# A conv-gated trunk on one core: four plain tiles instead of five in each channel mixer, and its first splits moved

## The chip, the cores and the metric

The kernel runs on one core of a Trainium2 chip. The metric is the device time of one execution in microseconds (us).

## The reference

Two layers. Each has a token mixer (layer 0: a chunked mLSTM with gates; layer 1: attention over a band of chunks; both beside attention over a memory) and then a channel mixer, which is where the change lies. All in float32, x being 512 tokens by 1024, `D_FF` 2816 = 22 tiles of 128:

```python
def conv_ffn(h, w_up, conv_w, conv_b, w_down):
    u, g = jnp.split(h @ w_up, 2, axis=-1)
    g = causal_dwconv(g, conv_w, conv_b)
    return (jax.nn.silu(g) * u) @ w_down
...
for l in range(DEPTH):
    ...
    x = x + jnp.concatenate([mix_out, mem_out], axis=-1) @ w_out
    x = x + conv_ffn(rmsnorm(x, norm_ffn_g[l]), ffn_w_up[l], ffn_conv_w[l], ffn_conv_b[l], ffn_w_down[l])
return rmsnorm(x, final_g)
```

## The kernel before

**Products.** x is held transposed, 8 tiles of 128 rows by 512 tokens. A float32 product is made of three TensorE matmuls on a high and a low part of each operand (`mm3`, L194 to L196: high by high, high by low, low by high). A *split* (`split`, L140 and L141) makes the parts: ACT casts the high part, DVE subtracts it from the source for the low part. Raw weights go into three buffers `wr`, their parts into `wh0`, `wl0` and so on in turn.

**The channel mixer** (`channel_mixer`, `ChannelMixer`) computes, for each of the 22 tiles of `D_FF`, a gate and an up product, the convolution on the gate, SiLU, and the product of both; the result is split and kept as `hid`. The first `PLAIN` tiles are *plain*: 24 matmuls for the gate and 24 for the up product, each 512 columns wide. The other tiles are *block* tiles (`later`, `step`): gate and up together as one 2 by 2 block product made of seven half-size products, 12 matmuls of 256 columns each, on sums of weight blocks (class `Forms`) and of blocks of x (method `forms`). The results are combined by copies out of PSUM (L834, L842) and additions on DVE (L845, L857). The products of a step stand in this order: a11, a12, s2, then a down unit, s1, s3, then a second down unit, a22, s4; a11, s2, s3 and a22 share the PSUM bank r1.

**Down units.** The down projection is cut into 32 *units* (`down_products`: four tiles of `hid` onto one tile of x, 12 matmuls of 512 columns into a bank with tag `tr`; ACT copies it out, L777, and GpSimd adds it in DRAM). `UNITS` says which units stand beside which tile: 0 to 3 behind the last plain tile, one each beside the block tiles 5 to 8, two beside each from 9 on.

**The norm** runs beside the first plain tile (`Norm.finish`): squares of x are summed, the sum is split, L299 sums over the rows on TensorE, and L301 to L308 make the row of factors. The first `UNSCALED` = 3 plain tiles take x without that row and scale the result; `forms` meanwhile makes the scaled x, its splits (`ready`) and the sums of its blocks (`sums`).

**Order.** The order of instructions on each engine is set by a scheduler, except for the block tiles from the first step on (a stretch of manual order on PE, ACT and DVE) and for instructions that are *pinned* (`pin`), which keep program order. Each engine works its queue in order. `weave` says how far `forms` advances beside a plain tile, in sixteenths.

Of the kernel before, what the change touches and what calls it, by code (L numbers as in the profile page):

```python
# [10 lines left out]
F32R = mybir.dt.float32r  # L11
# [5 lines left out]
P = 128  # L17
D = 1024
S = 512
# [20 lines left out]

PLAIN, UNSCALED, GROUP, LAST = 5, 3, 4, 6
UNITS = {PLAIN - 1: (0, 1, 2, 3), 5: (None, 4), 6: (None, 5), 7: (None, 6), 8: (None, 7)}
UNITS.update((j, (2 * j - 10, 2 * j - 9)) for j in range(9, 21))

H = S // 2
# [7 lines left out]
def trunk(  # L55
# [34 lines left out]
    def sb(tag, shape, dtype=F32):  # L90
        count[0] += 1
        return pool.tile(shape, dtype, tag=tag, name=f"{tag}{count[0]}", bufs=bufs[tag])

    def ps(tag):
        count[0] += 1
        return psum.tile([P, S], F32, tag=tag, name=f"p{tag}{count[0]}", bufs=pbufs[tag])
# [42 lines left out]
    def split(hi, lo, src, on_act=True, pinned=False):  # L139
        high = A.copy(hi, src) if on_act else V.tensor_copy(hi, src)  # L140
        low = V.tensor_tensor(out=lo, in0=src, in1=f(hi), op=ALU.subtract)  # L141
        if pinned:
            pin(high)
            pin(low)
# [13 lines left out]
    turn = [0]  # L158
# [26 lines left out]
    def weights(*args):  # L185
        return parts(load(*args))

    def rows(w, c0, n, k0=0, k1=None):
        k1 = k1 if k1 is not None else w.shape[0] // P
        return w[k0 * P : k1 * P, c0 : c0 + n].rearrange("(k p) c -> p k c", p=P)  # L190
# [4 lines left out]
        nc.tensor.matmul(o, lh, rl, start=False, stop=False, skip_group_check=more)  # L195
        nc.tensor.matmul(o, ll, rh, start=False, stop=last, skip_group_check=more)  # L196

    def project(w, c0, act, tag="mm"):


        n = len(act)
        wh, wl = weights(rows(w, c0, P), n, P)
        o = ps(tag)
        for k in range(n):
            mm3(o, wh[:, k, :], wl[:, k, :], act[k][0], act[k][1], k == 0, k == n - 1)
            yield
        return o

    def run(gen):
        while True:  # L210
            try:
                next(gen)
            except StopIteration as end:
                return end.value
# [10 lines left out]
    def weave(job, filler, each, lead=0):  # L225

        due = lead
        for n in chain([0], job):
            due += each if n is None else each * n
            while due >= 1:  # L230
                due -= 1
                next(filler, None)
# [43 lines left out]
    class Norm:  # L276
# [14 lines left out]
        def finish(self):  # L291


            parts = [sb("t", [P, S], F32R) for _ in range(2)]
            split(*parts, self.acc)
            yield 7.4
            o = ps("sc")
            for i, part in enumerate(parts):
                nc.tensor.matmul(o, onesr, part, start=i == 0, stop=i == 1)  # L299
            v, r, t = sb("rb", [P, S]), sb("t", [P, S]), sb("t", [P, S])  # L300
            A.activation(t, o, AF.Ln, scale=1.0 / D, bias=eps)  # L301
            V.tensor_scalar(v, o, 1.0 / D, EPS, op0=ALU.mult, op1=ALU.add)
            A.activation(r, t, AF.Exp, scale=-0.5)
            A.activation(t, r, AF.Square)
            yield 4
            V.scalar_tensor_tensor(t, t, -0.5, v, op0=ALU.mult, op1=ALU.mult)
            self.row = sb("rb", [P, S])
            V.scalar_tensor_tensor(self.row, t, 1.5, r, op0=ALU.add, op1=ALU.mult)  # L308
# [138 lines left out]
    with tc.manual_schedule(engines={mybir.EngineType.PE, mybir.EngineType.Activation, mybir.EngineType.DVE}):  # L447

        w = ps("mm")
# [215 lines left out]
    class ChannelMixer:  # L665
# [35 lines left out]
        def plain(self, j):  # L701
            scale = self.norm.row if j < UNSCALED else None
            act = self.act if j < UNSCALED else self.ready
            gate = project(self.w, DFF + j * P, act)
            up = project(self.w, j * P, act, "sc")
            if self.norm.row is None:
                both = pair_of(gate, up)
                weave(self.norm.finish(), both, 1)
                og, ou = yield from both
                scale = self.norm.row  # L710
            else:
                og = yield from gate
                ou = None
            acc = sb("t", [P, S])
            src = og
            if scale is not None:
                src = sb("t", [P, S])
                V.tensor_tensor(out=src, in0=og, in1=scale, op=ALU.mult)
            self.last_tap(j, acc, src)
            for _ in self.taps(j, acc, src):  # L720
                pass
            A.activation(acc, acc, AF.Silu)
            if scale is not None:
                V.tensor_mul(acc, acc, scale)
            if ou is None:
                ou = yield from up
            V.tensor_tensor(out=acc, in0=ou, in1=acc, op=ALU.mult)
            self.keep(acc)

        def forms(self):  # L730

            for j in range(KT):
                V.scalar_tensor_tensor(
                    xT[j], xT[j], self.gain[:, j : j + 1], self.norm.row, op0=ALU.mult, op1=ALU.mult
                )
                hi, lo = sb("u", [P, S], F32R), sb("u", [P, S], F32R)
                split(hi, lo, xT[j])
                self.ready.append((hi, lo))
                yield
            self.sums = []  # L740
            for k in range(KT // 2):
                b1, b2 = xT[k], xT[k + KT // 2]
                forms = []
                ta, tb = sb("t", [P, S]), sb("t", [P, S])
                for o, x, y in (
                    (ta[:, :H], b1[:, H:], b1[:, :H]),
                    (ta[:, H:], b2[:, H:], ta[:, :H]),
                    (tb[:, :H], b2[:, H:], b1[:, H:]),
                    (tb[:, H:], b2[:, :H], ta[:, H:]),
                ):  # L750
                    V.tensor_tensor(out=o, in0=x, in1=y, op=ALU.subtract)
                for t in (ta, tb):
                    for h in (t[:, :H], t[:, H:]):
                        both = sb("u", [P, S], F32R)
                        split(both[:, :H], both[:, H:], h)
                        forms.append(both)
                self.sums.append(forms)
                yield

# [3 lines left out]
            g, jj = divmod(q, KT // 2)  # L763
            return load(rows(ffn_w_down[self.l], 2 * jj * P, 2 * P, GROUP * g, GROUP * (g + 1)), GROUP, 2 * P)

        def down_products(self, u):
            g, j = divmod(u, KT)
            w = self.down[u // 2]
            o = ps("tr")
            c = slice(u % 2 * P, (u % 2 + 1) * P)  # L770
            for k in range(GROUP):
                mm3(o, w[0][:, k, c], w[1][:, k, c], *self.hid[GROUP * g + k], k == 0, k == GROUP - 1)
            return j, o

# [25 lines left out]

        def t(self, i):

            return [(p[i - 1][:, :H], p[i - 1][:, H:]) for p in self.sums]

        def later(self):


            prep, tail = Forms(self, PLAIN), None
            prep.split_up()
            prep.sums()  # L810
            prep.split_second()
            prep.sum_third()
            prep.split_sums()
            prep.sum_fourth()
            prep.split_down()
            prep.split_gate()
            with tc.manual_schedule(
                engines={mybir.EngineType.PE, mybir.EngineType.Activation, mybir.EngineType.DVE}
            ):
                for j in range(PLAIN, FT):  # L820
                    self.beside()
                    tail, prep = self.step(j, prep, Forms(self, j + 1) if j + 1 < FT else None, tail)
            for part in (tail.last_block, tail.first_tap, tail.second_tap, tail.third_tap, tail.gated, tail.split):
                part()
# [133 lines left out]
    def channel_mixer(l, act, norm, gain, beside):  # L958

        mixer = ChannelMixer(l, act, norm, gain, beside)  # L960
        forms = mixer.forms()
        run(mixer.plain(0))
        skips = -(turn[0] + 1) % 3
        for j in range(1, UNSCALED):
            turn[0] += j <= skips
            weave(mixer.plain(j), forms, KT / (16.0 * (UNSCALED - 1)))
        until(lambda: len(mixer.ready) == KT, forms)
        mixer.buffers()
        for j in range(UNSCALED, PLAIN):
            units = UNITS.get(j, ())  # L970
            raws = {u // 2: mixer.load_down(u // 2) for u in units[::2]}
            weave(mixer.plain(j), forms, 4 / (16.0 * (PLAIN - UNSCALED)))
            for u in units:
                if u // 2 not in mixer.down:
                    mixer.down[u // 2] = parts(raws[u // 2])
                mixer.add(*mixer.down_products(u))
        run(forms)
        mixer.later()
        reload_x()
        return mixer.hid[FT - LAST :]  # L980

# [556 lines left out]
```

## Time and profile before

| | |
|---|---|
| runs | 1180.72, 1180.85, 1180.89 us (median 1180.85) |
| the profiled execution's own time | 1181.04 us |
| its span | 1179.3 us |
| granted TensorE clock, mean | 0.999 |
| PE busy | 1169.1 us, 99%, 7007 matmuls |
| DVE busy | 935.7 us, 79% |
| ACT busy | 725.8 us, 62% |

Rows of a timeline read: start, length, engine, line, operation, what is written from what with its size, and in brackets the idle time before it and what ended that. An instruction's length overlaps the next one's start, so what an engine can do in a row is told by the distance of the starts. The first channel mixer of layer 0 starts its plain tiles at about 275 us, that of layer 1 at about 830 us.

### The profile page before, as it was taken

How to read it: one execution, taken by the hardware profiler on the slowest of the kernel's cores; microseconds unless marked ns; L12 is line 12 of the kernel's file. 1: busy time of each engine (PE TensorE's matmuls, PEld its weight loads, DVE VectorE, ACT ScalarE, POOL GpSimd, SP SyncE). 2: the span in 40 equal slices, each digit the busy share in tenths (PEclk: the TensorE clock that was granted, in tenths of full speed). 3: DMA queues.
4: the chain of work that ended last, by engine and by line, in shares of the span. 5: the costliest groups of instructions: out<-in, count | busy, mean ns of one | idle time of the engine just before them, and what ended most of it. 6: DMA issues, size and time to landing. Idle time of an engine off the chain costs nothing.

```text
span 1179.3 us, 18676 instructions
## 1 busy us (share of the span) xinstructions
PE 1169.1 (99%) x7007; PEld 1034.2 (88%) x7007; DVE 935.7 (79%) x1688; ACT 725.8 (62%) x1294; POOL 129.9 (11%) x222
## 2 busy tenths in 40 slices
PE   9999999999999999999999999999999999999997
PEld 9988888888889999999888888888889999999986
DVE  6877788887978877777698888897897877777755
ACT  6548677654655655555666667776565655555545
POOL 1111101000021111111020000101001011111100
PEclk9999999999999999999999999999999999999999
DMA  8645325244266677765564312335426466666551
GB/s 299 208 109 134 94 55 152 76 139 121 90 166 163 164 164 162 164 148 129 150 200 125 90 54 85 106 102 177 139 90 153 108 143 144 143 143 141 123 158 72
DMA packets 200156, 158.64 MB, mean 135 GB/s; under 512 B 8344, under 2 KB 179838, under 8 KB 200066
## 3 DMA queue, kind: packets, MB, share of 16 engines
q1 hardware_dynamic: 183906, 119.74, 34.6%
q0 software_dynamic: 15584, 36.67, 16.4%
q8 instruction: 55, 0.90, 0.3%
q10 hardware_dynamic: 576, 1.05, 0.2%
q14 instruction: 35, 0.29, 0.1%
HBM read 128.89 MB, written 32.46 MB: 137 GB/s over the span
## 4 chain that ended last, share of the span: by engine, by line
PE 94%; DVE 3%; ACT 1%; issue 0%; DMA 0%; SPq 0%; POOL 0%; ACTq 0%; POOLq 0%; DVEq 0%
PE pmm L194 18%; PE pmm L195 18%; PE pmm L196 18%; PE ptr L195 6%; PE ptr L194 6%; PE ptr L196 6%; PE psc L195 5%; PE psc L196 5%; PE psc L194 5%; PE psc L544 2%; PE ptr L1365 1%; PE ptr L1386 1%; PE ptr L1387 1%; PE ptr L627 1%; PE ptr L613 0%; DVE pt L141 0%
## 5 line engine op out<-in xcount | busy, mean ns | idle before, releaser
L194 PE MATMUL pmm<-u,wh 128*128 128x512 f32 (+1 forms) x968 | 333.2, 345 | 0.4 <-ACT u L140 0.2
L196 PE MATMUL pmm<-u,wl 128*128 128x512 f32 (+1 forms) x968 | 330.8, 342 | 0.0
L195 PE MATMUL pmm<-u,wh 128*128 128x512 f32 (+1 forms) x968 | 330.5, 342 | 0.0
L141 DVE TENSOR_TENSOR wl<-wr,wh 128x1024 fp32r<-128x1024 f32 (+3 forms) x172 | 199.6, 1162 | 101.8 <-ACT wh L140 101.4
L140 ACT CAST wh<-wr 128x1024 fp32r<-128x1024 f32 (+3 forms) x172 | 172.0, 1002 | 92.7 <-PE pmm L195 39.0
L196 PEld LDWEIGHTS pmm<-u,wl 128*128 128x128 f32 x968 | 181.9, 188 | 20.6
L194 PEld LDWEIGHTS pmm<-u,wh 128*128 128x128 f32 x968 | 181.8, 188 | 19.3 <-ACT u L140 1.1
L195 PEld LDWEIGHTS pmm<-u,wh 128*128 128x128 f32 x968 | 182.0, 188 | 18.5 <-DVE u L141 0.5
L194 PE MATMUL ptr<-u,wh 128*128 128x512 f32 x272 | 106.7, 392 | 0.0
L195 PE MATMUL ptr<-u,wh 128*128 128x512 f32 x272 | 106.5, 392 | 0.0
L196 PE MATMUL ptr<-u,wl 128*128 128x512 f32 x272 | 105.8, 389 | 0.0
L778 POOL DMA_DIRECT2D xspill<-t x64 | 55.6, 869 | 447.3 <-ACT t L777 437.5
L141 DVE TENSOR_TENSOR fl<-pt,fh 128x512 fp32r<-128x512 f32 x102 | 70.3, 689 | 11.2 <-ACT fh L140 8.5
L194 PE MATMUL pmm<-u,fh 128*128 128x256 f32 x272 | 75.4, 277 | 0.0
L195 PE MATMUL pmm<-u,fh 128*128 128x256 f32 x272 | 75.2, 276 | 0.0
L196 PE MATMUL pmm<-u,fl 128*128 128x256 f32 x272 | 75.2, 276 | 0.0
L195 PE MATMUL psc<-u,wh 128*128 128x256 f32 (+1 forms) x232 | 75.1, 324 | 0.0
L196 PE MATMUL psc<-u,wl 128*128 128x256 f32 (+1 forms) x232 | 75.1, 324 | 0.0
L194 PE MATMUL psc<-u,wh 128*128 128x256 f32 (+1 forms) x232 | 75.0, 324 | 0.0
L140 ACT CAST fh<-pt 128x512 fp32r<-128x512 f32 x102 | 62.7, 615 | 13.5 <-DVE pt L888 13.3
L950 ACT ACTIVATE t<-t 128x512 f32<-128x512 f32 x34 | 21.5, 632 | 79.2 <-DVE t L685 79.2
L777 ACT COPY t<-ptr 128x512 f32<-128x512 f32 x64 | 37.6, 587 | 51.6 <-PE ptr L196 51.6
(335 smaller groups left out, 2540.3 us busy)
## 6 DMA issues: line engine op xcount, KB each, us to landing
wr<-in_ffn_w_up_dram SPq DMA_DIRECT2D x54, 512.0 KB, 5.0
wr<-in_ffn_w_down_dram SPq DMA_DIRECT2D x38, 512.0 KB, 4.1
pt<-in_ffn_w_up_dram SPq DMA_DIRECT2D x34, 512.0 KB, 6.9
xspill<-t POOLq DMA_DIRECT2D x64, 256.0 KB, 4.7
wr<-in_a_w_in_dram SPq DMA_DIRECT2D x20, 512.0 KB, 3.8
wr<-in_w_kv_dram SPq DMA_DIRECT2D x12, 512.0 KB, 4.0
xspill<-fh POOLq DMA_DIRECT2D x16, 256.0 KB, 2.6
xspill<-fl POOLq DMA_DIRECT2D x16, 256.0 KB, 3.0
```

Of the source, the lines that this page charges most:

```text
L140: high = A.copy(hi, src) if on_act else V.tensor_copy(hi, src)
L141: low = V.tensor_tensor(out=lo, in0=src, in1=f(hi), op=ALU.subtract)
L194: nc.tensor.matmul(o, lh, rh, start=first, stop=False, skip_group_check=more)
L195: nc.tensor.matmul(o, lh, rl, start=False, stop=False, skip_group_check=more)
L196: nc.tensor.matmul(o, ll, rh, start=False, stop=last, skip_group_check=more)
L544: nc.tensor.matmul(o, a, b, start=first and i == 0, stop=i == 1)
L627: nc.tensor.matmul(o2, vs[a][:, 2 * hp + h, :], p[h][:, a, :], start=i == 0, stop=i == 3)
L777: A.copy(t, o)
L778: G.dma_start(xspill[j], t, accum_op=ALU.add)
L950: A.activation(self.acc, self.acc, AF.Silu)
L1365: nc.tensor.transpose(tp[:, b * P : (b + 1) * P], es[T, h][:, b * P : (b + 1) * P], ident)
L1386: nc.tensor.matmul(o2[:, s * P :], w, hi_at(pts[h], s, s, TT - s), start=s == 0, stop=False)
```

## The change

`PLAIN` goes from 5 to 4: each layer has one plain tile less and one block tile more (tile 4, which has no down unit). Units 0 to 3 stand beside plain tile 3, the last; as they need its `hid`, units 0 and 1 do three of their four tiles of `hid` first, and the fourth afterwards. The split of the up weights of plain tile 0 and of the norm's sum are pinned. The preparation of the first block tile (its up weights, its weight sums, the second form) is put ahead of the last block sums of x, and these take two splits of 512 columns instead of four of 256. The turn of the weight buffers is shifted by one to suit.

```diff
-PLAIN, UNSCALED, GROUP, LAST = 5, 3, 4, 6
+PLAIN, UNSCALED, GROUP, LAST = 4, 3, 4, 6
 UNITS = {PLAIN - 1: (0, 1, 2, 3), 5: (None, 4), 6: (None, 5), 7: (None, 6), 8: (None, 7)}
 UNITS.update((j, (2 * j - 10, 2 * j - 9)) for j in range(9, 21))
...
         nc.tensor.matmul(o, lh, rl, start=False, stop=False, skip_group_check=more)
         nc.tensor.matmul(o, ll, rh, start=False, stop=last, skip_group_check=more)
-    def project(w, c0, act, tag="mm"):
+    def project(w, c0, act, tag="mm", pinned=False):
         n = len(act)
-        wh, wl = weights(rows(w, c0, P), n, P)
+        wh, wl = parts(load(rows(w, c0, P), n, P), pinned=pinned)
         o = ps(tag)
         for k in range(n):
             mm3(o, wh[:, k, :], wl[:, k, :], act[k][0], act[k][1], k == 0, k == n - 1)
...
             parts = [sb("t", [P, S], F32R) for _ in range(2)]
-            split(*parts, self.acc)
+            split(*parts, self.acc, pinned=True)
             yield 7.4
             o = ps("sc")
             for i, part in enumerate(parts):
...
             scale = self.norm.row if j < UNSCALED else None
             act = self.act if j < UNSCALED else self.ready
             gate = project(self.w, DFF + j * P, act)
-            up = project(self.w, j * P, act, "sc")
+            up = project(self.w, j * P, act, "sc", self.norm.row is None)
             if self.norm.row is None:
                 both = pair_of(gate, up)
                 weave(self.norm.finish(), both, 1)
...
                 ):
                     V.tensor_tensor(out=o, in0=x, in1=y, op=ALU.subtract)
                 for t in (ta, tb):
-                    for h in (t[:, :H], t[:, H:]):
-                        both = sb("u", [P, S], F32R)
-                        split(both[:, :H], both[:, H:], h)
-                        forms.append(both)
+                    hi, lo = sb("u", [P, S], F32R), sb("u", [P, S], F32R)
+                    split(hi, lo, t)
+                    forms += [(hi[:, c], lo[:, c]) for c in (slice(0, H), slice(H, S))]
                 self.sums.append(forms)
                 yield
...
             g, jj = divmod(q, KT // 2)
             return load(rows(ffn_w_down[self.l], 2 * jj * P, 2 * P, GROUP * g, GROUP * (g + 1)), GROUP, 2 * P)
-        def down_products(self, u):
+        def down_products(self, u, k0=0, k1=GROUP, o=None):
             g, j = divmod(u, KT)
             w = self.down[u // 2]
-            o = ps("tr")
+            o = o or ps("tr")
             c = slice(u % 2 * P, (u % 2 + 1) * P)
-            for k in range(GROUP):
+            for k in range(k0, k1):
                 mm3(o, w[0][:, k, c], w[1][:, k, c], *self.hid[GROUP * g + k], k == 0, k == GROUP - 1)
             return j, o
...
         def t(self, i):
-            return [(p[i - 1][:, :H], p[i - 1][:, H:]) for p in self.sums]
-
-        def later(self):
+            return [p[i - 1] for p in self.sums]
+
+        def later(self, forms):
             prep, tail = Forms(self, PLAIN), None
             prep.split_up()
             prep.sums()
             prep.split_second()
+            run(forms)
             prep.sum_third()
             prep.split_sums()
             prep.sum_fourth()
...
         mixer = ChannelMixer(l, act, norm, gain, beside)
         forms = mixer.forms()
         run(mixer.plain(0))
-        skips = -(turn[0] + 1) % 3
+        skips = -(turn[0] + 2) % 3
         for j in range(1, UNSCALED):
             turn[0] += j <= skips
             weave(mixer.plain(j), forms, KT / (16.0 * (UNSCALED - 1)))
...
         for j in range(UNSCALED, PLAIN):
             units = UNITS.get(j, ())
             raws = {u // 2: mixer.load_down(u // 2) for u in units[::2]}
-            weave(mixer.plain(j), forms, 4 / (16.0 * (PLAIN - UNSCALED)))
+            weave(mixer.plain(j), forms, 3 / (16.0 * (PLAIN - UNSCALED)))
+            started = {}
             for u in units:
                 if u // 2 not in mixer.down:
                     mixer.down[u // 2] = parts(raws[u // 2])
-                mixer.add(*mixer.down_products(u))
-        run(forms)
-        mixer.later()
+                if u < 2:
+                    started[u] = mixer.down_products(u, 0, GROUP - 1)[1]
+                if u == 1:
+                    for v, o in started.items():
+                        mixer.add(*mixer.down_products(v, GROUP - 1, GROUP, o))
+                if u >= 2:
+                    mixer.add(*mixer.down_products(u))
+        mixer.later(forms)
         reload_x()
         return mixer.hid[FT - LAST :]
```

How the instructions move is shown at three places; numbers behind names count buffers in program order.

**PE, plain tiles 0 and 1 of layer 0**, behind L299's two matmuls: `pmm_2964` is tile 0's gate, `psc_3005` its up product (weights `wh_3001`, `wl_3002`), `pmm_3052` tile 1's gate (weights `wh_3048`, `wl_3049`). PE's queue before:

```order
L195 MATMUL pmm_2964<-u_2951,wh_2960 128x512
L196 MATMUL pmm_2964<-u_2950,wl_2961 128x512
L194 MATMUL psc_3005<-u_2794,wh_3001 128x512
L195 MATMUL psc_3005<-u_2795,wh_3001 128x512
L196 MATMUL psc_3005<-u_2794,wl_3002 128x512
L194 MATMUL psc_3005<-u_2803,wh_3001 128x512
```

The kernel before goes on with the up product. PE's queue at the same place after:

```order
L195 MATMUL pmm_2964<-u_2951,wh_2960 128x512
L196 MATMUL pmm_2964<-u_2950,wl_2961 128x512
L194 MATMUL pmm_3052<-u_2794,wh_3048 128x512
L195 MATMUL pmm_3052<-u_2795,wh_3048 128x512
L196 MATMUL pmm_3052<-u_2794,wl_3049 128x512
L194 MATMUL pmm_3052<-u_2803,wh_3048 128x512
L195 MATMUL pmm_3052<-u_2804,wh_3048 128x512
L196 MATMUL pmm_3052<-u_2803,wl_3049 128x512
L194 MATMUL psc_3005<-u_2794,wh_3001 128x512
L195 MATMUL psc_3005<-u_2795,wh_3001 128x512
L194 MATMUL pmm_3052<-u_2812,wh_3048 128x512
L195 MATMUL pmm_3052<-u_2813,wh_3048 128x512
```

Tile 1's gate now stands ahead of tile 0's up product: six of its matmuls, two of the up product, five more of the gate, then the remaining 22 of the up product. In layer 1 fourteen matmuls of tile 1's gate stand ahead.

**ACT at the same place** (L288 and L326 are the norm's squares and the scaling of x, L301 to L304 the norm's row). ACT's queue before:

```order
L140 COPY wh_3001<-wr_2999 128x1024
L288 ACTIVATE t_2907<-fl_2372 128x512
L326 ACTIVATE u_2910<-fl_2372,cols_451 128x512
L288 ACTIVATE t_2947<-fl_2374 128x512
L326 ACTIVATE u_2950<-fl_2374,cols_451 128x512
L140 COPY t_2954<-rb_2792 128x512
L301 ACTIVATE t_2991<-psc_2986,eps 128x512
L140 COPY wh_3048<-wr_3046 128x1024
L303 ACTIVATE t_2990<-t_2991 128x512
L304 ACTIVATE t_2991<-t_2990 128x512
```

Before, `wh_3001` was cast among the squares. ACT's queue there after:

```order
L288 ACTIVATE t_2947<-fl_2374 128x512
L326 ACTIVATE u_2950<-fl_2374,cols_451 128x512
L140 COPY t_2954<-rb_2792 128x512
L301 ACTIVATE t_2991<-psc_2986,eps 128x512
L140 COPY wh_3048<-wr_3046 128x1024
L303 ACTIVATE t_2990<-t_2991 128x512
L304 ACTIVATE t_2991<-t_2990 128x512
L140 COPY wh_3001<-wr_2999 128x1024
L692 ACTIVATE t_3033<-t_3034,cols_799 128x512
```

The cast of tile 0's up weights, `wh_3001`, moves from ahead of the last squares to behind L304; `wh_3048` stands behind L301 in both. On DVE the low part `wl_3002` moves accordingly, from behind an addition of x (L658) to behind L308. In layer 1 the cast of tile 1's gate stands ahead of the last square.

**PE, from the down units to the first block tile of layer 0**: `ptr_` are units, `u_3352` and `u_3353` the parts of the last plain tile's `hid`, `pmm_3479` the block tile's first product (weights `wh_3431`, `wl_3432`). Before, where tile 5 is the first block tile, with `pmm_3571`:

```order
L195 MATMUL ptr_3514<-u_3343,wh_3494 128x512
L196 MATMUL ptr_3514<-u_3342,wl_3495 128x512
L194 MATMUL pmm_3571<-u_3066,wh_3535 128x256
L195 MATMUL pmm_3571<-u_3067,wh_3535 128x256
L196 MATMUL pmm_3571<-u_3066,wl_3536 128x256
L194 MATMUL pmm_3571<-u_3083,wh_3535 128x256
```

The last unit was complete ahead of the block tile. PE's queue there after:

```order
L196 MATMUL ptr_3370<-u_3232,wl_3357 128x512
L194 MATMUL ptr_3360<-u_3352,wh_3356 128x512
L194 MATMUL ptr_3370<-u_3352,wh_3356 128x512
L194 MATMUL pmm_3479<-u_3066,wh_3431 128x256
L195 MATMUL pmm_3479<-u_3067,wh_3431 128x256
L196 MATMUL pmm_3479<-u_3066,wl_3432 128x256
L194 MATMUL pmm_3479<-u_3083,wh_3431 128x256
L195 MATMUL pmm_3479<-u_3084,wh_3431 128x256
L196 MATMUL pmm_3479<-u_3083,wl_3432 128x256
L194 MATMUL pmm_3479<-u_3115,wh_3431 128x256
L195 MATMUL ptr_3360<-u_3353,wh_3356 128x512
L196 MATMUL ptr_3360<-u_3352,wl_3357 128x512
```

All four units stood ahead of the first block tile; now 20 matmuls of units do, and the other 28 come within its first product. On DVE the last sums of x (L751, L141) stand between the block tile's steps; in layer 1 the low split of the first of them (`u_9654`) stands behind the addition L845:

```order
L751 TENSOR_TENSOR t_9647<-fh_8536 128x256
L751 TENSOR_TENSOR t_9648<-fl_8544,fh_8536 128x256
L751 TENSOR_TENSOR t_9647<-fl_8544,t_9647 128x256
L845 TENSOR_TENSOR t_9685<-t_9685,pmm_9683 128x256
L751 TENSOR_TENSOR t_9648<-fl_8544,t_9647 128x256
L888 TENSOR_TENSOR pt_9443<-pt_9442 128x512
L141 TENSOR_TENSOR u_9654<-t_9647,u_9653 128x512
```

That addition takes the block tile's second product from PE.

## The prediction

> **What bounds the kernel now.** I read the page first, then the busy time by stretches through the first channel mixer, then the timelines of its first plain tiles and its first block tile.
>
> ```profile
> span 1179.3 us, 18676 instructions
> PE 1169.1 (99%) x7007; PEld 1034.2 (88%) x7007; DVE 935.7 (79%) x1688; ACT 725.8 (62%) x1294; POOL 129.9 (11%) x222
> PE 94%; DVE 3%; ACT 1%; issue 0%; DMA 0%; SPq 0%; POOL 0%; ACTq 0%; POOLq 0%; DVEq 0%
> ```
>
> PE is busy 1169.1 of 1179.3 us and holds 94% of the chain that ended last. So a matmul taken out is worth its pitch, and a wait put in front of a matmul costs its full length, since nothing else is late. The stretches (columns: PE, PEld, DVE, ACT, POOL busy, granted clock, DMA share, GB/s) show how much room the engines have that feed PE:
>
> ```profile
> 286.40:297.30 10.90, 10.90 (x49) 9.02 (x49) 10.81 (x16) 7.41 (x9) 0.00 (x0) 1.00 0.27 79
> 319.10:330.00 10.90, 10.90 (x49) 8.92 (x48) 10.90 (x26) 7.90 (x14) 0.00 (x0) 1.00 0.47 142
> 330.00:341.00 11.00, 11.00 (x50) 9.10 (x49) 8.35 (x12) 5.86 (x10) 2.60 (x3) 1.00 0.64 148
> 341.00:353.30 12.30, 12.30 (x99) 11.81 (x97) 7.89 (x11) 6.92 (x12) 3.51 (x5) 1.00 0.72 171
> ```
>
> In the plain tiles (the first two rows) DVE has no room: 10.81 and 10.90 of 10.90. The 11 us of down units behind the last plain tile (third row) are where DVE catches up: it is done with the first block tile's preparation before PE gets there. PE has no gap in any of these stretches.
>
> **What the change takes out.** One plain tile in each layer becomes a block tile.
>
> ```profile
> 286.45 0.39 PE L194 MATMUL pmm<-u,wh 128*128 128x512 f32 x1
> 297.33 0.39 PE L194 MATMUL pmm<-u,wh 128*128 128x512 f32 x1
> ...
> 338.19 0.39 PE L194 MATMUL ptr<-u,wh 128*128 128x512 f32 x1
> 340.90 0.28 PE L194 MATMUL pmm<-u,wh 128*128 128x256 f32 x1
> 353.19 0.28 PE L194 MATMUL pmm<-u,wh 128*128 128x256 f32 x1
> ```
>
> A plain tile takes 297.33 - 286.45 = 10.88 us (48 matmuls at 0.2267). A unit takes 340.90 - 338.19 = 2.71. The first block tile with one unit takes 353.19 - 340.90 = 12.29, so a bare block tile takes 12.29 - 2.71 = 9.58 at most, and 84 matmuls at half a plain pitch give 9.52. The exchange saves 10.88 - 9.52 = 1.36 us a layer, **2.72 us** in all. The units are the same 32 in each layer. All else in the change is a question of waits.
>
> **Place A: the first and second plain tile of layer 0.** Pinning the norm's second split and the up split in program order puts the up split of tile 0 behind the norm's activations (the ACT order shown above), and PE's order now takes the gate of tile 1 first.
>
> ```profile
> 279.83 0.63 PE L299 MATMUL psc<-t,onesr 128*128 128x512 f32 x2
> ...
> 280.99 0.39 PE L194 MATMUL psc<-u,wh 128*128 128x512 f32 x1
> ...
> 269.65 1.05 ACT L140 CAST wh<-wr 128x1024 fp32r<-128x1024 f32 x1 [2.75 <-PE pmm L195]
> ...
> 280.50 0.69 ACT L301 ACTIVATE t<-psc,eps 128x512 f32<-128x512 f32 x1 [2.49 <-PE psc L299]
> 281.08 1.04 ACT L140 CAST wh<-wr 128x1024 fp32r<-128x1024 f32 x1
> ...
> 282.68 0.63 ACT L304 ACTIVATE t<-t 128x512 f32<-128x512 f32 x1
> ...
> 270.73 1.23 DVE L141 TENSOR_TENSOR wl<-wr,wh 128x1024 fp32r<-128x1024 f32 x1 [0.21 <-ACT wh L140]
> ...
> 282.15 1.23 DVE L141 TENSOR_TENSOR wl<-wr,wh 128x1024 fp32r<-128x1024 f32 x1 [0.24 <-ACT wh L140]
> ...
> 284.07 0.69 DVE L308 SCALAR_TENSOR_TENSOR rb<-t,t 128x512 f32<-128x512 f32 x1
> 284.80 0.69 DVE L718 TENSOR_TENSOR t<-pmm,rb 128x512 f32<-128x512 f32 x1
> ```
>
> Today, at 280.99, PE goes on with tile 0's up product, whose weights were split at 269.65 and 270.73, in idle time. In the new order the next matmul is tile 1's gate, with the weights that ACT splits at 281.08, behind L301, which itself waits for L299 on PE. That split ends at 282.12; with 0.05 for the start (DVE, released by it too, starts 0.03 behind it) PE waits 282.12 + 0.05 - 280.99 = 1.18. Two matmuls (0.45) later it needs the low part, which DVE ends at 282.15 + 1.23 = 283.38: another 0.80. Together **1.98 us** in layer 0. The up weights then come behind L304 (high part about 283.3 to 284.3, low part about 284.8 to 286.0), while PE has the other gate matmuls. In layer 1 the order has 14 gate matmuls whose weights are split ahead of the norm, so only a short restart (below) is due there. The moved low split has a second price: 1.13 us of DVE pass from idle time into the stretch where DVE has no room.
>
> **Place B: the first block tile.** Its preparation no longer stands behind 11 us of units. DVE's pitches:
>
> ```profile
> 317.96 1.22 DVE L141 TENSOR_TENSOR wl<-wr,wh 128x1024 fp32r<-128x1024 f32 x1
> 319.09 0.75 DVE L141 TENSOR_TENSOR u<-t,u 128x256 fp32r<-128x256 f32 x2
> ...
> 320.37 0.42 DVE L751 TENSOR_TENSOR t<-fh 128x256 f32<-128x256 f32 x1
> 320.70 0.42 DVE L751 TENSOR_TENSOR t<-fl,fh 128x256 f32<-128x256 f32 x1
> ...
> 321.37 0.68 DVE L141 TENSOR_TENSOR u<-t,u 128x512 fp32r<-128x512 f32 x1
> 321.97 0.42 DVE L751 TENSOR_TENSOR t<-fl,t 128x256 f32<-128x256 f32 x1
> ...
> 326.31 0.75 DVE L685 SCALAR_TENSOR_TENSOR t<-pmm,cols,t 128x511 f32<-128x511 f32 x1
> 326.97 0.42 DVE L751 TENSOR_TENSOR t<-fl,t 128x256 f32<-128x256 f32 x1
> ...
> 332.31 1.22 DVE L141 TENSOR_TENSOR wl<-wr,wh 128x1024 fp32r<-128x1024 f32 x1
> ```
>
> That is 1.13 for 1024 columns, 0.60 for 512 (0.66 with a scalar column, L685 and L733), 0.335 for 256. From L308's end to the block's up low split, before's order has 84 instructions: 10 of 1.13, 21 of 0.60, 18 of 0.66, 32 of 0.335, and three L718 at 0.60: 48.3 us, so from 284.80 to 333.1; the trace has the end of that split at 333.53. After's order has 64: 9 of 1.13, 27 of 0.60, 16 of 0.66, 12 of 0.335, or 41.0. (The wider splits are in this: two of 256 cost 0.67, one of 512 costs 0.60, so eight pairs save 0.5 a layer.) 284.80 + 41.0 + 0.1 = 325.9. PE comes there after 168 plain matmuls and 20 of the units: 280.99 + 1.98 + 188 x 0.2267 + 2 x 0.113 = 325.8. So DVE and PE arrive together: a wait of 0.1 to 0.4, I take **0.2**. In layer 1, where place A holds PE up less, DVE is later:
>
> ```profile
> 838.52 0.69 DVE L308 SCALAR_TENSOR_TENSOR rb<-t,t 128x512 f32<-128x512 f32 x1
> 839.25 0.69 DVE L718 TENSOR_TENSOR t<-pmm,rb 128x512 f32<-128x512 f32 x1
> 835.44 0.39 PE L194 MATMUL psc<-u,wh 128*128 128x512 f32 x1
> ```
>
> After L308 (about 839.13) now come tile 0's low split (1.13) and 61 more instructions, 38.2 by the same pitches: 878.5. PE has 186 matmuls and two half ones from 835.44, and one restart of 0.2: 835.44 + 0.2 + 42.17 + 0.2 = 878.0. Wait: 0.5 to 0.8, I take **0.7**.
>
> Two waits inside the first block tile come on top. It has no unit, while the first block tile of before has one between the product s3 and the product a22, both in bank r1.
>
> ```profile
> 343.90 0.42 DVE L845 TENSOR_TENSOR t<-t,pmm 128x256 f32<-128x256 f32 x1 [0.71 <-PE pmm L196]
> 345.19 0.37 ACT L834 COPY t<-pmm 128x256 f32<-128x256 f32 x1 [2.34 <-PE pmm L196]
> ...
> 370.79 0.28 PE L196 MATMUL psc<-u,wl 128*128 128x256 f32 x1
> 371.11 0.38 PE L194 MATMUL pmm<-u,wh 128*128 128x256 f32 x1
> 371.33 0.28 PE L195 MATMUL pmm<-u,wh 128*128 128x256 f32 x1
> ```
>
> Without the unit, a22 waits for s3's last matmul to drain (0.28 - 0.11 = 0.17), for the copy L834 (0.37) and a start (0.05): 0.6, in both layers **1.2**. And in layer 1 the last sums of x have their low split behind L845, which waits for PE's second product to end: L845, L751, L888 and the split take 0.05 + 0.335 + 0.335 + 0.6 + 0.69 = 2.0 from then, while PE comes to it in ten half matmuls, 1.13: **0.87**. In layer 0 that split stands ahead of L845. The rows at 370.79 show what reuse of a bank costs when only a copy is late: 371.11 - 370.79 = 0.32 for 0.11, so 0.21. I count seven such restarts (the units' two banks, once in each layer; s4 and the next tile; the layer-1 gate), **1.5** in all. The second matmul after that wait also comes late (371.33 - 371.11 = 0.22, for 0.11): 0 to 0.2 at each of the 14 waits named, I take half, **0.7**. On weights that wait: the Trainium skill ("TensorE: Matmul & The Clock Gate", section "Step-by-step: what each phase is for") says that the queue pulls weight loads ahead of running matmuls; by that the 0.7 would be 0, and the row at 371.11, where the next pitch doubles, speaks against it, if weakly.
>
> **The sum.** 1.98 + 0.2 + 0.7 + 1.2 + 0.87 + 1.5 + 0.7 = 7.15 of waits, less 2.72: +4.4 us. The profiled execution took 1181.04 (its span and 1.7 around it), so 1185.4; the median of the runs is 0.19 below it: **1185.2**.
>
> **The rivals.** *The cover holds* (nothing waits, only matmuls are saved): -2.72, so 1178.1, faster. For it: DVE and PE meet within 0.2 us in layer 0. Against it: place A is fixed by order, and nothing in the trace lets ACT end that split before 282.12. It decides only if the weights of tile 1's gate could be ready ahead of L301. 5%. *Only place A waits*, B's small waits being hidden by a DVE that runs ahead: 1180.85 - 2.72 + 1.98 = 1180.1, the same within what can be told. Against it: the two a22 waits need no late DVE. 9%. *B's preparation comes late by a transfer*: the up weights of the first block tile are issued only when a raw buffer comes free at the last plain tile's up split:
>
> ```profile
> wr<-in_ffn_w_up_dram SPq DMA_DIRECT2D x54, 512.0 KB, 5.0
> ```
>
> Landing takes 5.0 at the median, and the slack I find is about 7 us; a landing of 8 or 9 with the units' weights beside it adds some 2.2 in one layer or both, 1187.4 to 1189.6. 7%. *The clock falls*: it is 1.00 in each stretch above, but none of them has a wait as long as place A's. Were those two waits taken for idleness, and the 22 matmuls of tile 0's up product that stand next in a row run at twice 0.2267, this would add 5.0: 1190.2. The Trainium skill (the same page, "Part 1: The HAM clock gate") has the clock halve after an idle window of about 3.4 us, for about as long; an estimate from it is 1.7 us lost, and 1.18 and 0.80 with matmuls between them would not bring it about. 4%. The forecast case keeps 75%.
>
> **How the numbers follow.** About 0.2%, or 2.4 us, is what a measurement of this kernel can tell from no change: faster is below 1178.5, slower above 1183.2. The forecast's own range drops the terms DVE decides (0.2, 0.7, 0.87) and the 0.7 of second matmuls at its low end: 1185.2 - 2.5 = 1182.7; at its high end the doubtful ones come out at twice: 1187. With the transfers' case partly in: 1182.4 to 1187.6. Faster 0.05; same 0.10 (the second rival and the low tail); slower 0.85.
>
> **What would show it.** In the profile after: PE x7079 (84 for 48 matmuls, twice), if all records are there; two gaps on PE right behind L299's tile in layer 0, near 1.2 and 0.8, released by ACT L140 and DVE L141; DVE's low split of tile 0's up weights behind L308; in the first block tile of each layer a gap of some 0.6 ahead of a22, released by ACT L834, and in layer 1 one of some 0.9 released by a DVE split. It would be wrong if PE shows no gap near 281, if the gaps at the first block tiles sum to under 1.5 or over 7 us, or if gaps appear elsewhere.

## The result, and the profile after

The changed kernel takes 1187.17 us (median of 6, 1186.82 to 1188.84) against 1180.87 for the kernel before: 6.3 us slower, a ratio of 1.0051 (95% interval 1.0041 to 1.0061). The profiled execution took 1187.08.

The page of the changed kernel, its lines on the span, the engines and the chain:

```profile
span 1185.3 us, 18825 instructions
PE 1171.0 (99%) x7079; PEld 1037.1 (87%) x7079; DVE 945.3 (80%) x1692; ACT 728.0 (61%) x1292; POOL 129.6 (11%) x222
PE 89%; DVE 7%; ACT 3%; issue 1%; POOL 0%; ACTq 0%; DVEq 0%; POOLq 0%
```

The 72 matmuls more are there, and the span is 6.0 longer. PE's share of the last chain fell from 94 to 89%; DVE now has 7 and ACT 3. Place A on the timelines of PE, ACT and DVE (the bracket gives idle time and what ended it):

```profile
280.64 0.40 PE L196 MATMUL pmm<-u,wl 128*128 128x512 f32 x1
282.11 0.50 PE L194 MATMUL pmm<-u,wh 128*128 128x512 f32 x1 [1.07 <-ACT wh L140]
282.44 0.40 PE L195 MATMUL pmm<-u,wh 128*128 128x512 f32 x1
283.37 0.50 PE L196 MATMUL pmm<-u,wl 128*128 128x512 f32 x1 [0.53 <-DVE wl L141]
...
281.02 1.03 ACT L140 CAST wh<-wr 128x1024 fp32r<-128x1024 f32 x1
...
283.16 1.03 ACT L140 CAST wh<-wr 128x1024 fp32r<-128x1024 f32 x1
...
282.09 1.22 DVE L141 TENSOR_TENSOR wl<-wr,wh 128x1024 fp32r<-128x1024 f32 x1 [0.24 <-ACT wh L140]
```

The starts are 1.47 and 0.93 apart where 0.227 is the pitch: waits of 1.24 and 0.70. (The bracket counts from the end of the record before, which the pitch overlaps; I go by starts.) The casts of tile 1's gate (281.02) and of tile 0's up weights (283.16) stand where the order said. The first block tile, layer 0, then layer 1:

```profile
325.87 0.28 PE L195 MATMUL pmm<-u,wh 128*128 128x256 f32 x1
326.41 0.39 PE L196 MATMUL pmm<-u,wl 128*128 128x256 f32 x1 [0.27 <-DVE wl L141]
...
339.67 0.28 PE L196 MATMUL pmm<-u,wl 128*128 128x256 f32 x1
340.54 0.39 PE L194 MATMUL pmm<-u,fh 128*128 128x256 f32 x1 [0.59 <-ACT t L834]
340.76 0.28 PE L195 MATMUL pmm<-u,fh 128*128 128x256 f32 x1
...
350.78 0.40 PE L194 MATMUL ptr<-u,wh 128*128 128x512 f32 x1
...
882.21 0.39 PE L196 MATMUL pmm<-u,wl 128*128 128x256 f32 x1 [0.90 <-DVE wl L141]
...
894.28 0.39 PE L195 MATMUL pmm<-u,fh 128*128 128x256 f32 x1 [0.62 <-DVE u L141]
...
898.05 0.39 PE L194 MATMUL pmm<-u,fh 128*128 128x256 f32 x1 [0.52 <-ACT t L834]
```

By starts these are 0.43 for the up weights' low part in layer 0 and 1.07 in layer 1, 0.76 and 0.68 ahead of a22 (behind the copy L834), and 0.79 for the last sums of x behind L845. Each matmul behind a wait is followed late: 340.76 - 340.54 = 0.22, for 0.113. The weight loads (PEld) around the same wait show what is late:

```profile
339.56 0.19 PEld L196 LDWEIGHTS pmm<-u,wl 128*128 128x128 f32 x1
...
340.53 0.19 PEld L194 LDWEIGHTS pmm<-u,fh 128*128 128x128 f32 x1 [0.79 <-ACT t L834]
340.64 0.19 PEld L195 LDWEIGHTS pmm<-u,fh 128*128 128x128 f32 x1
```

In the stream, the load for the matmul at 339.67 starts at 339.56, beside the matmul before it. The load for the matmul that waited starts with that matmul (340.53 and 340.54) and not during the wait, and so it is at every wait over 0.125 us in these mixers, in each run's profile. The 0.11 thus looks like a load that no earlier matmul covers.

One thing is new: from 340.54 to the first down unit at 350.78 stand 84 half matmuls, 9.52 us at the usual pitch, but they take 10.24. Of the 0.72, 0.27 are two late second matmuls and a small restart; 0.45 is spread evenly, the pitch being 0.1185 instead of 0.1134. In layer 1 the 84 from 898.05 on take 10.08, with one late second matmul and the same 0.45.

Summed over both channel mixers, and against the same sums in the kernel before: 6.3 in waits, 1.2 in late second matmuls, 1.2 in the slow pitch and excesses smaller than 0.1, together 8.7; less 2.72 for the plain tiles this is 6.0, what the span grew by.

### The profile page after: what moved, and what is told of

Same layout as the page of the kernel before. It is cut to its first block, busy times and chain, and to the rows that moved or that the text cites. A ratio compares the mean times of both kernels' runs of the same rounds, so it can differ in the third digit from the quotient of the medians.

```text
span 1185.3 us, 18825 instructions
## 1 busy us (share of the span) xinstructions
PE 1171.0 (99%) x7079; PEld 1037.1 (87%) x7079; DVE 945.3 (80%) x1692; ACT 728.0 (61%) x1292; POOL 129.6 (11%) x222
## 4 chain that ended last, share of the span: by engine, by line
PE 89%; DVE 7%; ACT 3%; issue 1%; POOL 0%; ACTq 0%; DVEq 0%; POOLq 0%
PE pmm L194 17%; PE pmm L196 17%; PE pmm L195 17%; PE ptr L195 6%; PE ptr L194 6%; PE ptr L196 6%; PE psc L195 5%; PE psc L194 5%; PE psc L196 5%; PE psc L544 2%; DVE wl L141 1%; DVE u L141 1%; PE ptr L1371 1%; PE ptr L1392 1%; PE ptr L1393 1%
## 5 line engine op out<-in xcount | busy, mean ns | idle before, releaser
L141 DVE TENSOR_TENSOR wl<-wr,wh 128x1024 fp32r<-128x1024 f32 (+3 forms) x170 | 197.4, 1162 | 93.7 <-ACT wh L140 93.3
L140 ACT CAST wh<-wr 128x1024 fp32r<-128x1024 f32 (+3 forms) x170 | 169.6, 1000 | 78.5 <-PE pmm L195 33.8
L141 DVE TENSOR_TENSOR fl<-pt,fh 128x512 fp32r<-128x512 f32 x108 | 74.4, 689 | 9.3 <-ACT fh L140 6.5
L194 PE MATMUL pmm<-u,fh 128*128 128x256 f32 x288 | 80.2, 279 | 1.2 <-ACT t L834 1.1
L195 PE MATMUL pmm<-u,fh 128*128 128x256 f32 x288 | 79.9, 277 | 0.6 <-DVE u L141 0.6
L196 PE MATMUL pmm<-u,fl 128*128 128x256 f32 x288 | 79.7, 277 | 0.0
L140 ACT CAST fh<-pt 128x512 fp32r<-128x512 f32 x108 | 66.2, 615 | 15.3 <-DVE pt L888 15.3
L195 PE MATMUL psc<-u,wh 128*128 128x256 f32 (+1 forms) x224 | 71.2, 318 | 0.0
L194 PE MATMUL psc<-u,wh 128*128 128x256 f32 (+1 forms) x224 | 71.1, 318 | 0.0
L196 PE MATMUL psc<-u,wl 128*128 128x256 f32 (+1 forms) x224 | 71.1, 317 | 0.0
```

The lines of the kernel that those rows point to most:

```text
L194: nc.tensor.matmul(o, lh, rh, start=first, stop=False, skip_group_check=more)
```

## The experiments

Differences are to the kernel before as run beside them; the change itself stands at +6.30.

**Without the pin on tile 0's up split.**

```diff
-up = project(self.w, j * P, act, "sc", self.norm.row is None)
+up = project(self.w, j * P, act, "sc")
```

> The changed kernel without the pin on plain tile 0's up split (the norm's pin stays). The cast of those weights goes back ahead of the last squares, and PE takes tile 0's up product first again. My theory (place A is the cost of this one pin): the waits of 1.24 and 0.70 near 281 us and the two slow second matmuls behind them go, 2.2 in all; in layer 1 the 0.79 behind L845 goes too, since DVE has 1.13 less to do there; the first block's low split waits 0.5 to 0.7 in both layers. Sum about -2.9: 1184.3. Rival (DVE is the bound from the norm to the first block tile, so time given back at 281 us is lost again at the block): 1186.5 to 1187.2, with a wait for the first block's low split of over 2 us in layer 0.

1185.08 us, +4.06 (ratio 1.0035, 1.0022 to 1.0048): 2.2 of the 6.3 go, not 2.9. The two waits go, but another takes their place. ACT and PE in layer 0:

```profile
277.28 1.05 ACT L140 CAST wh<-wr 128x1024 fp32r<-128x1024 f32 x1 [5.19 <-DMA wr<-in_ffn_w_up_dram]
...
280.22 0.62 ACT L140 CAST t<-rb 128x512 fp32r<-128x512 f32 x1 [0.75 <-DVE rb L289]
...
280.89 0.50 PE L299 MATMUL psc<-t,onesr 128*128 128x512 f32 x1 [0.66 <-ACT t L140]
281.62 0.50 PE L299 MATMUL psc<-t,onesr 128*128 128x512 f32 x1 [0.23 <-DVE t L141]
```

Without the pin the queue of ACT has the cast of tile 2's gate weights ahead of the norm's last square, and ACT stands 5.2 us for that transfer; L299 comes 0.8 and 0.5 late. The first block's low part waits 0.95 there instead of 0.43 (the rival had over 2). So layer 0 gains only 0.3 us, and nearly all that the edit brings comes from layer 1, which had no place A. There the cast ahead of the norm's last square is tile 1's gate, which waits for no transfer; the low part waits 0.67 instead of 1.07, the 0.79 behind L845 is gone, and the mixer's waits over 0.125 fall from 3.2 to 1.8. That fits the second price that the prediction names, 1.13 us of DVE moved into the stretch where it has no room.

**The pin alone, on the kernel before.**

> The kernel before, five plain tiles, with nothing but the pin on plain tile 0's up split. PE's and ACT's queues around 281 us in layer 0 are then those of the changed kernel. My theory: the two waits of 1.24 and 0.70 and two slow second matmuls come, +2.2 in layer 0, +0.2 in layer 1, all else covered by the 11 us of units: 1183.2 to 1183.6, and in those executions in which the granted clock halves behind place A some 1.6 more. Rival (the waits at place A belong to the four-tile schedule, and the pin alone costs nothing): 1181.0.

1185.32, +4.75 (1.0046, 1.0032 to 1.0059): 1.7 us more than expected. PE's list of waits, line, releaser, sum, number, longest:

```profile
PE pmm L194 <- ACT wh L140: 2.1, 2, 1.1
...
PE pmm L196 <- DVE wl L141: 1.1, 2, 0.5
```

There are two of each: with five plain tiles place A opens in layer 1 as well, by starts 1.24 and 0.70 again. I had taken layer 1's order from the four-tile kernel, where the cast of tile 1's gate happens to stand ahead of the norm. So the pin is the cause of place A, whatever `PLAIN` is.

**Unit 3 into the first block tile.**

```diff
-UNITS = {PLAIN - 1: (0, 1, 2, 3), 5: (None, 4), ...
+UNITS = {PLAIN - 1: (0, 1, 2), 4: (None, 3), 5: (None, 4), ...
```

> The changed kernel with unit 3 moved from beside the last plain tile into the first block tile, between s3 and a22. My theory: the waits before a22 (0.76 and 0.68, each with 0.11 at its second matmul) go, and with the unit's 512-wide matmuls there PE's weight loads win back their lead, so that the stretch of half matmuls at 0.118 to 0.119 instead of 0.1134 behind the wait (about 100 of them a layer, some 0.5 each) is short; in layer 1 the wait behind L845 may grow by 0.2. Sum about -2.4: 1184.8. Rival 1 (the slow pitch has nothing to do with the unit): only the waits go, -1.6 + 0.2: 1185.8, pitch at 0.118 still seen to 354 us. Rival 2 (PE comes earlier at everything else and waits as long elsewhere): 1187.

1186.23, +5.21 (1.0047, 1.0034 to 1.0059). It is nearest to the first rival's number, but not by its mechanism: both a22 waits went, and so did layer 0's slow pitch (0.1134 from 345 us on). Given back were waits of 0.21 and 0.49 ahead of s3 in the next tile, 0.93 in place of 0.79 behind L845, and, in the profiled execution, a clock that halved behind place A (below).

**`PLAIN` = 4 alone, on the kernel before.**

> The kernel before with PLAIN = 4 and nothing else of the change. My theory: the change's other edits are what keeps the loss small; without them DVE does the last sums of x and four-way splits ahead of the first block's weights with no 11 us of spare time, so waits of 3 to 5 at the units and of 1 to 2 at the block in each layer, 16 in all: -2.7 + 17: about 1195. Rival (the other edits bring nothing or cost all of it): 1178 to 1187.

1199.99, +18.97 (1.0159, 1.0145 to 1.0172). Its largest waits:

```profile
PE ptr L196 <- DVE wl L141: 4.6, 1, 4.6
PE psc L196 <- DVE wl L141: 3.7, 1, 3.7
```

DVE is what is late, as place B has it. The change's other edits together bring back 12.7 of these 19 us; which of them do isn't shown, and two, the pin and the wider splits, cost time. The waits sum to 13.8 where I had 16. What takes the time above my number is a clock that I had no term for: some 20 matmuls come 0.2 late at half the clock behind the two waits shown, and 15 half matmuls 0.1 late behind two more in layer 1, of 1.11 and 0.92 us with two matmuls between them: 5.8 in all. The same two waits in layer 0 left the clock at 1.00.

**Sums split in four again.**

```diff
-hi, lo = sb("u", [P, S], F32R), sb("u", [P, S], F32R)
-split(hi, lo, t)
-forms += [(hi[:, c], lo[:, c]) for c in (slice(0, H), slice(H, S))]
+for h in (t[:, :H], t[:, H:]):
+    both = sb("u", [P, S], F32R)
+    split(both[:, :H], both[:, H:], h)
+    forms.append((both[:, :H], both[:, H:]))
```

> The changed kernel with the sums of x's blocks split in four pieces of 256 columns again instead of two of 512; all else as changed. Theory A (by the queues: the scheduler, which puts the split of the first block's up weights by what stands before it, then places it ahead of more of the last splits): the waits for that low part (0.43 in layer 0, 1.07 in layer 1) and the 0.79 behind L845 go, waits of about 1.0 at the units of layer 1 come; place A stays at 2.2 and the a22 waits at 0.7 each; -1.2 to -2: 1185.2 to 1186. Rival (DVE's 0.5 us more in each layer, eight pairs at 0.07, comes on top of the waits for the first block, since DVE is what ends last there): +0.5 to +1.0: 1187.7 to 1188.2.

1185.64, +4.71 (1.0039, 1.0026 to 1.0052): the wider splits cost 1.6 us, though each saves DVE time. The two queues of PE show why: in layer 0, with four pieces, all 48 matmuls of the four units stand ahead of the matmul that needs the block's low weights; with two, that matmul comes after 20 of them. In layer 1 it comes after 24 instead of 18. The low-part wait in layer 0 is gone, in layer 1 it falls from 1.07 to 0.10 (with 0.22 and 0.52 at units), and the 0.79 is gone.

**No unit in the second block tile either,** and, on the kernel before, **none in its first.**

```diff
-5: (None, 4), 6: (None, 5)
+5: (None, None), 6: (4, 5)
```

> The changed kernel with unit 4 moved from block tile 5 to block tile 6, which then has two, so that tile 5 has none either. My theory: tile 5 gets the same wait before a22 as tile 4 (0.7 to 1.0, with 0.11 at the second matmul) and a 0.2 at s4, and the pitch of 0.118 to 0.119 that begins behind tile 4's wait goes on through tile 5 to the first 512-wide unit, in tile 6: another 70 to 90 half matmuls at 0.005 more, 0.4. Sum 1.3 to 1.5 a layer: +2.7 to +3.0: 1189.9 to 1190.2. Rival (the slow pitch ends by itself some 12 us after the wait): pitch back at 0.1134 in tile 5 before its own wait; +1.8 to +2.2: 1189.2.

> The kernel before with unit 4 moved from its first block tile (5) to the next, so that nothing stands between s3 and a22 there; no other wait precedes it. My theory: 0.65 to 0.76 ahead of a22 (a matmul's end, the copy L834, a start), 0.11 at the second matmul, and then the next 83 half matmuls, up to the first 512-wide unit, at 0.118 to 0.119 instead of 0.1134, 0.45 in all: 1.25 to 1.35 a layer, +2.5 to +2.7: 1183.5. Rival (the slow pitch needs the earlier waits and the late DVE of the changed kernel): only the waits, +1.7: 1182.6, with the pitch at 0.1134 within ten matmuls.

> The last kernel once more, for a second profile: in the first, the wait ahead of a22 (0.62 in both layers) was followed by 83 half matmuls at 0.1185 in layer 0, and by the usual 0.1134 in layer 1. If the slow pitch is fixed by the instructions, layer 0 is slow and layer 1 is not again; if it hangs on the moment at which the wait ends, the pattern can differ.

On the changed kernel 1189.73, +8.71, so 2.4 more than the change, between the theory's number and the rival's: a wait of 0.92 ahead of a22 in tile 5 of each layer, and in both layers the slow pitch from tile 4 runs on to the unit in tile 6. On the kernel before 1182.76, +2.19 (1.0018, 1.0009 to 1.0026), again between. Its timeline, a22's first matmul and the first unit's behind it, 60 half matmuls apart (I had counted 83), for layer 0 and layer 1:

```profile
347.99 0.39 PE L194 MATMUL pmm<-u,fh 128*128 128x256 f32 x1 [0.46 <-ACT t L834]
...
355.23 0.39 PE L194 MATMUL ptr<-u,wh 128*128 128x512 f32 x1
...
903.30 0.38 PE L194 MATMUL pmm<-u,fh 128*128 128x256 f32 x1 [0.46 <-ACT t L834]
...
910.21 0.40 PE L194 MATMUL ptr<-u,wh 128*128 128x512 f32 x1
```

And in a second profile of the same kernel:

```profile
347.95 0.38 PE L194 MATMUL pmm<-u,fh 128*128 128x256 f32 x1 [0.46 <-ACT t L834]
...
354.86 0.40 PE L194 MATMUL ptr<-u,wh 128*128 128x512 f32 x1
...
902.99 0.38 PE L194 MATMUL pmm<-u,fh 128*128 128x256 f32 x1 [0.46 <-ACT t L834]
...
910.23 0.40 PE L194 MATMUL ptr<-u,wh 128*128 128x512 f32 x1
```

The same matmuls behind the same wait take 7.24 and 6.91 in the first profile, 6.91 and 7.24 in the second (1182.36 us). So the slow pitch needs neither the late DVE nor the earlier waits, and it isn't fixed by the instructions: one wait brings it on and the next does not. What decides that stays open. In the traces it ended with a down unit, where 512 columns leave 0.227 for each weight load, or by itself within about ten matmuls.

**The changed kernel once more.**

> The changed kernel once more, for a second profile: the same waits within 0.1 us; the pitch behind the a22 waits at 0.118 to 0.119 in both layers if it is fixed by the instructions; the granted clock at 1.00 or 0.50 behind place A, the time being some 1.6 longer in the second case.

1188.46 us, and the clock did fall. Busy times by stretches (PE first, the granted clock third from the end), and two matmuls of the second one:

```profile
283.00:284.00 1.00, 0.65 (x2) 0.59 (x3) 0.97 (x3) 1.00 (x2) 0.00 (x0) 0.82 0.00 0
284.00:285.00 1.00, 1.00 (x4) 0.71 (x4) 1.00 (x2) 0.17 (x1) 0.00 (x0) 0.50 0.38 111
285.00:286.00 1.00, 1.00 (x4) 0.81 (x3) 1.00 (x2) 0.00 (x0) 0.00 (x0) 0.50 1.03 308
286.00:287.00 1.00, 1.00 (x4) 0.81 (x3) 1.00 (x3) 0.55 (x1) 0.00 (x0) 0.50 0.39 115
...
284.13 0.63 PE L195 MATMUL pmm<-u,wh 128*128 128x512 f32 x1
284.56 0.63 PE L196 MATMUL pmm<-u,wl 128*128 128x512 f32 x1
```

From 283.7 on eight matmuls come 0.427 apart, 1.6 us lost. Those waits are the first profile's within 0.03, and there the clock held at 1.00. By its size the median of the change is without it; its slowest run, 1188.84, and this one have the time that it would give. Behind layer 0's a22 wait the pitch is 0.1185 again; behind layer 1's it is 0.1134, where the first profile had 0.1185. That brings little: PE is earlier at s3 of the next tile and waits 0.21 there, with 0.11 at its second matmul. So part of the slow pitch only stands in for such a wait.

**Three edits, and a fourth.** No pin, unit 3 in the first block tile, sums in four; then also tile 1's gate weights split, pinned, right behind the norm's sum. (The first also leaves out the norm's pin, which changes no queue; the second has it again, and turns the weight buffers as the kernel before does. Its main lines:)

```diff
 split(*parts, self.acc, pinned=True)
+if then:
+    then()   # splits plain tile 1's gate weights, pinned
 yield 7.4
```

> Three edits at once on the changed kernel: no pin on tile 0's up split, unit 3 in the first block tile, sums split in four. My theory (each wait goes with its cause and they add up): place A keeps the 1.3 and 0.2 that the run without the pin showed ahead of L299 in layer 0 (a cast of tile 2's gate weights waits for its transfer there), one wait of some 0.5 in each first block tile, no a22 wait, no low-split wait: 1181 to 1182. Rival (waits come back elsewhere as in the two runs before, each giving half of what was expected): 1183 to 1184.

> As the kernel with three edits, and in addition the split of plain tile 1's gate weights is pinned directly behind the split of the norm's sum, that is ahead of L301, where ACT and DVE stood idle for 2.5 us; its raw load is issued first. My theory: the cast of tile 2's gate weights then stands behind the norm, so that nothing waits near 280 us in layer 0; left are some 0.3 in layer 1's plain tiles and 0.5 to 0.9 in each first block tile, with 0.11 at each second matmul: 2.3 in all, less 2.72: 1180.3 to 1180.9, level with the kernel before or just faster. Rival (a load issued earlier takes the raw buffer of another, whose transfer is then late): a wait of 1 to 3 us named <-DMA in the plain tiles: 1182 to 1184.

1181.88, +0.95 (1.0005, 0.9996 to 1.0014) and 1182.02, +1.09 (1.0008, 1.0000 to 1.0017). The three edits take away 5.3 of the 6.3 us, as their theory had it; one at a time they took 2.2, 1.1 and 1.6. (The first one's profiled execution, 1184.22, is its slowest, with waits of 1.3 and 0.5 in the first token mixer that the changed kernel's profile hasn't; what is said here is of the channel mixers.) The fourth removed the waits near 280 us, as its theory had it, but against the three edits it has 0.29 more in layer 1's plain tiles and 0.2 more in its block tile, and the time didn't fall: it is over 1 us above its theory. It lies in its rival's range, but not by its mechanism: the waits for transfers in the plain tiles are ACT's (1.7 at most), and PE has none. Neither beats the kernel before: restarts of 0.2 to 0.44 in the last one's mixers (seven, two of them also in the kernel before), their late second matmuls, and about 1 us of slow pitches and small excesses, which its theory left out, use up the 2.72 us of the two plain tiles.

Two parts of the change have no effect of their own: with the preparation of the first block tile put behind the last sums of x again, or without the norm's pin, the queues of PE, ACT and DVE are the same but for buffer numbers.

## Why the prediction was right

Slower was forecast, 1185.2 in 1182.4 to 1187.6; it is 1187.17, by the mechanism given 75%. By its terms:

| term | forecast | measured |
|---|---|---|
| matmuls saved | -2.72 | x7079, as forecast |
| place A | 1.98 | 1.94 |
| low part of the first up weights | 0.2 + 0.7 | 0.43 + 1.07 |
| a22 behind L834 | 1.2 | 0.76 + 0.68 |
| behind L845 | 0.87 | 0.79 |
| seven short restarts | 1.5 | 0.43, at three of them; 0.22 at s2 in layer 1, not one of them |
| second matmul behind a wait | 0.7 | 1.2 |
| slow pitch behind a wait, and excesses under 0.1 | none | 1.2 |

Places, releasers and the larger sizes came out. The two steps that were mis-sized are the last two: I halved the second matmul's 0.11, which comes at every wait, and I had no term for a pitch that stays slow. Their 1.7 us are most of the distance from 1185.2 to 1187.2. The other misses nearly cancel, which is luck: the low parts came 0.6 dearer than forecast and the restarts 0.85 cheaper. By the rule of the Trainium skill on weight loads ("TensorE: Matmul & The Clock Gate", "Step-by-step: what each phase is for"), taken as the prediction took it, the second matmul would have cost nothing. The traces agree with the rule in a stream of matmuls (the load at 339.56) and disagree behind every wait (the load at 340.53).

Of the rivals, "the cover holds" and "only place A waits" are refuted by the rows above. No wait was named <-DMA at the first block tile, so the third didn't happen. The fourth, the clock, was argued wrongly: I held that 1.18 and 0.80 with matmuls between them would not bring it about, and in two of the six profiles with place A in layer 0 it did. That it held in the change's own profile is luck. The estimate from the Trainium skill (the same page, "Part 1: The HAM clock gate"), 1.7 us for a clock halved for 3.4, agrees with the 1.6 measured; its 3.4 us of idleness were not needed.

And the wider splits, which I counted as 0.5 a layer in DVE's favour, cost 1.6: I took the order as given and didn't ask which edit had put the block's first product that far ahead.

## What to carry to other kernels

Where TensorE has no gap, price a change by the waits that it opens, each from the queue order and the rows of the engine waited for; here 0.1 came on top of each for the second matmul, and up to 0.5 for a slow stretch behind it. Pinning an instruction moves everything that the scheduler had put around it: look for what now stands behind a wait on the same queue, in each layer apart. An edit that relieves the busy engine can still lose if the scheduler answers by starting the next consumer earlier.

## What the runs showed of the hardware

In the channel mixers, a matmul's weight load starts beside the matmul before it, but behind every wait over 0.125 us it starts with its own matmul, and the second matmul is 0.11 late at the full clock. After a wait, half-size matmuls sometimes go on at 0.1185 instead of 0.1134 for tens of matmuls, in one profile of a kernel behind one wait and in the next profile behind another. And two waits of 1.24 and 0.70 us with two matmuls between them were enough to halve the granted clock for about 3.4 us in some executions, and not in others with the same waits; two of 1.11 and 0.92 did it in one layer of a run and not in the other.
